# Projections that read their tokens alternately from two halves

## The chip, the cores and the metric

The kernel runs on one core of a Trainium2 chip. The metric is device time in microseconds (us). The engines are TensorE (PE, with its weight load PEld), VectorE (DVE), ScalarE (ACT), GpSimd (POOL) and SyncE (SP), which issues the DMAs. Matmuls read from SBUF and write to PSUM, which has eight banks; one bank holds 512 float32 columns on each of 128 partitions.

## The reference

Two layers of an encoder trunk on 256 tokens of width 2048, in float32. Layer 0 mixes tokens with RWKV-7 heads and an RG-LRU side by side; layer 1 uses sparse attention with low-rank queries and keys.

```python
for layer in range(DEPTH):
    if layer % 2 == 0:
        z = x @ ev_w_in[j]
        y_a = rwkv7_mix(z[..., :A_COLS], ...)
        y_b = rglru_mix(z[..., A_COLS:], ...)
        y = jnp.concatenate([y_a, y_b], axis=-1) @ ev_w_out[j]
    else:
        y = dsa_mix(x, od_w_in[j], ...) @ od_w_out[j]
    x = layer_norm(DN_ALPHA * x + y, ...)
    x = layer_norm(DN_ALPHA * x + conv_ffn(x, ...), ...)
    x = x + jax.nn.sigmoid(x @ ple_w_gate[layer]) * (p[layer] @ ple_w_proj[layer])
```

`rwkv7_mix` mixes each token with the one before it (`z + (token_shift(z) - z) * mu`), `rglru_mix` and `conv_ffn` run a causal convolution over four and three tokens. These are the places where the order of the tokens matters outside a matmul.

## The kernel before

Activations lie transposed: 128 features on the partitions, 256 tokens along the free axis (`S` = 256). A float32 value is split into a high part that fp32r holds and a residual, so an activation tile `hl` has 512 columns: high parts of tokens 0 to 255, then residuals of tokens 0 to 255 (`hl_split`, L135). Weights are split in the same way into `hi` and `lo` after each load (`wchunk`, L117): SP issues the load, ACT makes `hi`, DVE makes `lo`.

A product of one 128 x 128 weight block and one activation tile is made by `mm3` (L141) in one of two forms. The form with two matmuls (L149, L150) multiplies `hi` with all 512 columns and `lo` with the 256 high ones; the bank then holds two halves of 256 sums, which its reader adds. The form with three matmuls (`one=True`, L145 to L147) puts everything into one half. `gproj` (L171) runs over the blocks of one output block (16 for the width 2048, 44 for the feed-forward width), and `ordered` (L164) does the same in an order that `dodge` writes out for a few blocks (L169). All the large projections go through these: input and output projections of the mixers, the up and down projections of the feed-forward part (`ffn`, L376), the gate (`ple`, L464), the small projections of the attention layer (`small_proj`, L1345) and the projection of `p` (`ple_proj`, L427).

The banks are read by `evac` (L246: ACT copies one half to SBUF, DVE adds the other), `ln_set` and `ln_more` (L267, L276: DVE adds to the scaled residual stream), `ple_proj` (ACT scales), `ple` (a last tanh on ACT), `shifted` (L732: ACT scales by 1 - mu, DVE adds mu times the token before), `rglru` (L1023: ACT applies the last tap of the convolution and DVE the three others, all straight from the bank; later ACT applies Gelu to a second bank), `index_keys`, `low_rank` and `small_proj` in the attention layer (ACT copies).

In the even layer `stage1` and `stage2` of the RWKV heads are generators. A driver in `run` takes matmuls of other projections from `filler` whenever a stage yields, so that TensorE has work while short chains on DVE and ACT finish. Instructions run in the order of each engine's queue; semaphores that the tile framework places hold the dependencies. Attention's own products, the recurrent products of the RWKV heads and the block products of the RG-LRU are plain float32 matmuls that don't go through `mm3`.

Of the kernel before, what the change touches and what calls it, by code (L numbers as in the profile page):

```python
# [14 lines left out]
P = 128  # L15
D = 2048
S = 256
# [39 lines left out]
class Core:  # L57
# [77 lines left out]
    def hl_split(self, dst, src):  # L135
# [3 lines left out]
        nc.vector.tensor_tensor(dst[:, S:2 * S], src, dst[:, 0:S].bitcast(F32), op=ALU.subtract)  # L139

    def mm3(self, ps, hi, lo, hl, first, last, one=False):  # L141

        nc = self.nc
        if one:
            nc.tensor.matmul(ps[:, 0:S], hi, hl[:, 0:S], start=first, stop=False)  # L145
# [3 lines left out]
        nc.tensor.matmul(ps[:, 0:2 * S], hi, hl, start=first, stop=False)  # L149
        nc.tensor.matmul(ps[:, 0:S], lo, hl[:, 0:S], start=False, stop=last)  # L150

# [12 lines left out]
    def ordered(self, ps, hi, lo, hls, k0, order):  # L164

        for what, k in order[2 * k0:2 * k0 + 16]:
            c = slice((k - k0) * P, (k - k0 + 1) * P)
            out, w, x = (ps[:, 0:2 * S], hi, hls[k]) if what == "H" else (ps[:, 0:S], lo, hls[k][:, 0:S])
            self.nc.tensor.matmul(out, w[:, c], x, start=(what, k) == order[0], stop=(what, k) == order[-1], skip_group_check=True)  # L169
# [76 lines left out]
    def evac(self, ps, out):  # L246

        nc = self.nc
        t = self.t("ev")
        nc.scalar.copy(t, ps[:, S:2 * S])  # L250
        nc.vector.tensor_tensor(out, ps[:, 0:S], t, op=ALU.add)  # L251

# [14 lines left out]
    def ln_set(self, m, ps, hl):  # L267

        nc = self.nc
        s = self.sm[m] = self.ln_new(m)  # L270
        t = self.t("lnt")
        nc.vector.scalar_tensor_tensor(s, hl[:, 0:S].bitcast(F32), ALPHA, ps[:, 0:S], op0=ALU.mult, op1=ALU.add)
        nc.vector.scalar_tensor_tensor(t, hl[:, S:2 * S].bitcast(F32), ALPHA, ps[:, S:2 * S], op0=ALU.mult, op1=ALU.add)
        nc.vector.tensor_tensor(s, s, t, op=ALU.add)

    def ln_more(self, m, ps):  # L276

        s = self.sm[m]
        self.nc.vector.tensor_tensor(s, s, ps[:, 0:S], op=ALU.add)

# [146 lines left out]
    def ple_proj(self, l, wps, phl, half, pool=None):  # L427

        pps, pss = [], [None] * 2
        for m in range(8 * half, 8 * half + 8):  # L430
            wp = wps[m % 8 // 4]
            if pool is None:

                if m % 4 < 2:
                    pss[m % 2] = self.ps()
                ps, n = pss[m % 2], m % 4 // 2
            else:
                if m % 2 == 0:
                    ps = self.ps()
                n = m % 2  # L440
            pv = ps[:, n * S:(n + 1) * S]
            for k in range(2):
                o = ((m % 4) * 2 + k) * P
                self.mm3(pv, wp[0][:, o:o + P], wp[1][:, o:o + P], phl[k], k == 0, k == 1, True)
            if pool is None:
                t = self.t("sp")
                self.nc.scalar.mul(t, pv, 0.5)
                self.nc.sync.dma_start(self.spill[l][:, (m % 8) * S:(m % 8 + 1) * S], t)
            elif m % 2:
                pp = pool.tile([P, 2 * S], F32, tag="pp", name=self.nm("pp"), bufs=KD // 2)  # L450
                self.nc.scalar.mul(pp, ps, 0.5)
                pps += [pp[:, 0:S], pp[:, S:]]
        return pps
# [10 lines left out]
    def ple(self, l, pool, new, raws, emit):  # L464
# [7 lines left out]
        def finish(m, ps):  # L472
# [6 lines left out]
            if m == KD - 1:  # L479
                nc.scalar.activation(g, ps[:, 0:S], AF.Tanh, scale=0.5)  # L480
            else:
# [197 lines left out]
class Even:  # L679
# [343 lines left out]
    def rglru(self, j, yout):  # L1023
# [3 lines left out]
        xc = self.r1("xc")  # L1027
        A.activation(xc, ps[:, 0:S], AF.Identity, bias=k.v("bconv_b", j), scale=k.v("bconv3", j))
# [33 lines left out]
        g = self.r1("g")  # L1062
        A.activation(g, ps[:, 0:S], AF.Gelu_apprx_tanh)
        V.tensor_tensor(h, h, g, op=ALU.mult)
# [173 lines left out]
class Odd:  # L1238
# [31 lines left out]
    def index_keys(self):  # L1270
# [5 lines left out]
        z = k.t("kz")  # L1276
        A.copy(z, ps[:, 0:S])
        yield
# [28 lines left out]
    def low_rank(self, m0, n, gain, name, back=False):  # L1307
# [7 lines left out]
        for i in range(n):  # L1315
# [5 lines left out]
            z = zs[i]  # L1321
            A.copy(z, ps[:, 0:S])
            if i == 0:
# [21 lines left out]
    def small_proj(self, w, o, hls, out, scale=1.0):  # L1345
# [4 lines left out]
        for i in range(n):  # L1350
            k.mm3(ps, w[0][:, o + i * P:o + (i + 1) * P], w[1][:, o + i * P:o + (i + 1) * P], hls[i], i == 0, i == n - 1, True)
        nc.scalar.mul(out, ps[:, 0:S], scale)

# [263 lines left out]
```

## Time and profile before

| what | us |
|---|---|
| median of 3 runs | 2404.59 |
| lowest and highest | 2403.81 and 2405.13 |
| span of the profiled execution | 2404.5 |
| TensorE busy in it | 2382.8 |
| VectorE busy in it | 1773.9 |
| ScalarE busy in it | 1377.4 |

The even layer's mixer fills about the first 450 us, then come its output, the feed-forward part and the gate up to about 1340 us, the attention layer's mixer, and the second feed-forward part and gate up to the end. A line of the profile's list of groups gives the line of the kernel, the engine, the operation, the tile written and those read, the shape and the count; then the busy time in us, the mean duration of one in ns, and the engine's idle time just before them with what ended it. Durations of matmuls overlap, since matmuls are pipelined: how long one holds TensorE is read from the start of the next. L53 is the line of a helper through which many operations on DVE and ACT are issued, so these go by their tiles.

### The profile page before, as it was taken

Reading aid. Unit: us, or ns where it says so; the run is one execution under the profiler, and the core shown is the slowest. Engines: PE = TensorE matmul, PEld = TensorE weight load, DVE = VectorE, ACT = ScalarE, POOL = GpSimd, SP = SyncE. Lnnn points to the kernel's source line nnn. Section 1 sums busy time; section 2 is a strip of 40 time slices with the busy share of each in tenths; the row PEclk is TensorE's granted clock in tenths of the full one; section 3 lists DMA queues with packets and bytes.
Section 4 is the critical chain, followed back from the end, with each engine's and each line's share of the span. In section 5 each row is a group of like instructions: output and inputs, shape, how many; then the busy total and the mean of one; then the engine's idle time right before and its main releaser. Section 6 shows DMA issues by size and latency. Waiting matters only on the chain.

```text
span 2404.5 us, 40333 instructions
## 1 busy us (share of the span) xinstructions
PE 2382.8 (99%) x15064; PEld 2139.0 (89%) x15064; DVE 1773.9 (74%) x3598; ACT 1377.4 (57%) x2610; POOL 77.0 (3%) x73
## 2 busy tenths in 40 slices
PE   9999999999999999999999999999999999999999
PEld 8999999888888888888888998888888888888898
DVE  7788888887777777655579598887777777655587
ACT  6777776466555555443356567565555555444354
POOL 0011110000000000000000030000000000000000
PEclk9999999999999999999999999999999999999999
DMA  7444444556665666666666654646666666666665
GB/s 240 145 153 142 139 121 153 174 177 203 191 188 191 191 189 190 185 189 188 189 187 199 188 164 143 214 150 189 191 189 189 192 191 189 183 189 189 192 193 158
DMA packets 137588, 433.77 MB, mean 180 GB/s; under 512 B 16544, under 2 KB 29232, under 8 KB 137392
## 3 DMA queue, kind: packets, MB, share of 16 engines
q1 hardware_dynamic: 137392, 431.19, 57.8%
q8 instruction: 118, 1.93, 0.4%
q14 instruction: 78, 0.64, 0.1%
HBM read 426.65 MB, written 4.48 MB: 179 GB/s over the span
## 4 chain that ended last, share of the span: by engine, by line
PE 88%; DVE 4%; ACT 3%; DMA 3%; issue 1%; POOL 0%; SPq 0%; POOLq 0%; DVEq 0%; ACTq 0%
PE a L149 26%; PE pp L149 18%; PE a L150 13%; PE pp L150 9%; PE pp L145 4%; PE pp L146 4%; PE pp L147 3%; PE a L169 3%; PE a L875 2%; PE pp L169 1%; DMA raw<-evin 1%; ACT hi L53 1%; DVE lo L53 1%; DMA wr<-pg 1%; PE a L145 1%
## 5 line engine op out<-in xcount | busy, mean ns | idle before, releaser
L53 DVE TENSOR_TENSOR lo<-raw,hi 128x1024 fp32r<-128x1024 f32 (+3 forms) x1153 | 976.9, 862 | 464.6 <-ACT hi L53 462.5
L53 ACT CAST hi<-raw 128x1024 fp32r<-128x1024 f32 (+3 forms) x1153 | 840.3, 755 | 697.8 <-PE a L149 305.3
L149 PE MATMUL a<-x,hi 128*128 128x512 f32 x1768 | 619.1, 394 | 2.2 <-DVE x L333 2.2
L150 PE MATMUL a<-x,lo 128*128 128x256 f32 x1768 | 489.6, 277 | 0.0
L149 PEld LDWEIGHTS a<-x,hi 128*128 128x128 f32 x1768 | 331.3, 188 | 79.5 <-DVE x L333 2.9
L149 PE MATMUL pp<-x,hi 128*128 128x512 f32 x1112 | 391.6, 394 | 0.0
L150 PEld LDWEIGHTS a<-x,lo 128*128 128x128 f32 x1768 | 332.0, 188 | 0.3
L150 PE MATMUL pp<-x,lo 128*128 128x256 f32 x1112 | 308.0, 277 | 0.0
L149 PE MATMUL a<-g,hi 128*128 128x512 f32 x836 | 290.4, 394 | 0.0
L149 PEld LDWEIGHTS pp<-x,hi 128*128 128x128 f32 x1112 | 208.5, 188 | 48.5 <-ACT hi L53 0.2
L145 PE MATMUL pp<-x,hi 128*128 128x256 f32 x800 | 239.2, 300 | 1.5 <-ACT x L138 1.2
L150 PE MATMUL a<-g,lo 128*128 128x256 f32 x836 | 231.6, 277 | 0.0
L146 PE MATMUL pp<-x,hi 128*128 128x256 f32 x800 | 226.1, 283 | 0.9 <-DVE x L139 0.9
L147 PE MATMUL pp<-x,lo 128*128 128x256 f32 x800 | 225.9, 283 | 0.0
L392 DVE SCALAR_TENSOR_TENSOR cv<-u,vec_sb,cv 128x255 f32<-128x255 f32 x352 | 169.5, 482 | 64.1 <-ACT cv L389 58.2
L150 PEld LDWEIGHTS pp<-x,lo 128*128 128x128 f32 x1112 | 208.8, 188 | 0.2 <-DVE lo L53 0.2
L149 PEld LDWEIGHTS a<-g,hi 128*128 128x128 f32 x836 | 156.8, 188 | 36.5
L149 PE MATMUL pp<-g,hi 128*128 128x512 f32 x484 | 168.3, 394 | 0.0
L389 ACT ACTIVATE cv<-u,vec_sb 128x256 f32<-128x256 f32 x176 | 105.7, 601 | 93.0 <-DVE u L251 93.0
L150 PEld LDWEIGHTS a<-g,lo 128*128 128x128 f32 x836 | 156.8, 188 | 0.0
L145 PEld LDWEIGHTS pp<-x,hi 128*128 128x128 f32 x800 | 152.8, 191 | 2.9 <-ACT x L138 1.6
L146 PEld LDWEIGHTS pp<-x,hi 128*128 128x128 f32 x800 | 153.0, 191 | 2.1 <-DVE x L139 1.6
(439 smaller groups left out, 3734.9 us busy)
## 6 DMA issues: line engine op xcount, KB each, us to landing
raw<-up SPq DMA_DIRECT2D x347, 512.0 KB, 4.4
raw<-dn SPq DMA_DIRECT2D x160, 512.0 KB, 4.2
raw<-evin SPq DMA_DIRECT2D x85, 512.0 KB, 4.2
raw<-pg SPq DMA_DIRECT2D x54, 512.0 KB, 4.7
raw<-odout SPq DMA_DIRECT2D x32, 512.0 KB, 4.5
raw<-evout SPq DMA_DIRECT2D x16, 512.0 KB, 4.0
raw<-dn SPq DMA_DIRECT2D x32, 256.0 KB, 2.9
raw<-evout SPq DMA_DIRECT2D x16, 448.0 KB, 4.0
```

What stands on the lines that cost most here:

```text
L53: return getattr(self.eng, name)(*args, **kw)
L145: nc.tensor.matmul(ps[:, 0:S], hi, hl[:, 0:S], start=first, stop=False)
L146: nc.tensor.matmul(ps[:, 0:S], hi, hl[:, S:2 * S], start=False, stop=False)
L147: nc.tensor.matmul(ps[:, 0:S], lo, hl[:, 0:S], start=False, stop=last)
L149: nc.tensor.matmul(ps[:, 0:2 * S], hi, hl, start=first, stop=False)
L150: nc.tensor.matmul(ps[:, 0:S], lo, hl[:, 0:S], start=False, stop=last)
L169: self.nc.tensor.matmul(out, w[:, c], x, start=(what, k) == order[0], stop=(what, k) == order[-1], skip_group_check=True)
L389: nc.scalar.activation(y, u, AF.Identity, bias=self.v(f"cb{l}", j), scale=self.v(f"cw2{l}", j))
L392: nc.vector.scalar_tensor_tensor(y[:, d:], u[:, 0:S - d], self.v(f"cw{n}{l}", j), y[:, d:], op0=ALU.mult, op1=ALU.add)
L875: self.nc.tensor.matmul(ps[:, c * P:(c + 1) * P], lhs[:, c * P:(c + 1) * P], rhs(c), start=True, stop=True)
```

## The change

Three helpers give access patterns. `zip` makes a matmul read the 256 tokens of a half as 0, 128, 1, 129, and so on: the inner step is 128 elements with a count of two, the outer step one element. The tiles in SBUF keep their order. The matmul still writes its columns one after the other, so column 2b of a bank holds token b and column 2b + 1 token 128 + b. `unzip` reads a bank back in token order, all the even columns and then all the odd ones, and `nat` gives an SBUF tile the same shape.

```diff
+    def zip(self, ap):
+        if ap.shape[1] == S:
+            return ap.rearrange("p (q b) -> p b q", q=2)
+        return ap.rearrange("p (h q b) -> p h b q", h=2, q=2)
+    def unzip(self, ap):
+        return ap.rearrange("p (b q) -> p q b", q=2)
+    def nat(self, ap):
+        return ap.rearrange("p (q b) -> p q b", q=2)
...
-            nc.tensor.matmul(ps[:, 0:S], hi, hl[:, 0:S], start=first, stop=False)
-            nc.tensor.matmul(ps[:, 0:S], hi, hl[:, S:2 * S], start=False, stop=False)
-            nc.tensor.matmul(ps[:, 0:S], lo, hl[:, 0:S], start=False, stop=last)
+            nc.tensor.matmul(ps[:, 0:S], hi, z(hl[:, 0:S]), start=first, stop=False)
+            nc.tensor.matmul(ps[:, 0:S], hi, z(hl[:, S:2 * S]), start=False, stop=False)
+            nc.tensor.matmul(ps[:, 0:S], lo, z(hl[:, 0:S]), start=False, stop=last)
...
-        nc.tensor.matmul(ps[:, 0:2 * S], hi, hl, start=first, stop=False)
-        nc.tensor.matmul(ps[:, 0:S], lo, hl[:, 0:S], start=False, stop=last)
+        nc.tensor.matmul(ps[:, 0:2 * S], hi, z(hl), start=first, stop=False)
+        nc.tensor.matmul(ps[:, 0:S], lo, z(hl[:, 0:S]), start=False, stop=last)
...
-        nc.scalar.copy(t, ps[:, S:2 * S])
-        nc.vector.tensor_tensor(out, ps[:, 0:S], t, op=ALU.add)
+        nc.scalar.copy(self.nat(t), self.unzip(ps[:, S:2 * S]))
+        nc.vector.tensor_tensor(self.nat(out), self.unzip(ps[:, 0:S]), self.nat(t), op=ALU.add)
...
-        nc.vector.scalar_tensor_tensor(s, hl[:, 0:S].bitcast(F32), ALPHA, ps[:, 0:S], op0=ALU.mult, op1=ALU.add)
-        nc.vector.scalar_tensor_tensor(t, hl[:, S:2 * S].bitcast(F32), ALPHA, ps[:, S:2 * S], op0=ALU.mult, op1=ALU.add)
+        for o, c in ((s, slice(0, S)), (t, slice(S, 2 * S))):
+            nc.vector.scalar_tensor_tensor(self.nat(o), self.nat(hl[:, c].bitcast(F32)), ALPHA, self.unzip(ps[:, c]), op0=ALU.mult, op1=ALU.add)
...
-        nc.scalar.mul(out, ps[:, 0:S], self.omu[:, j:j + 1])
-        nc.vector.scalar_tensor_tensor(out[:, 1:], ps[:, 0:S - 1], k.v("mu", j), out[:, 1:], op0=ALU.mult, op1=ALU.add)
+        o, p, mu, h = k.nat(out), k.unzip(ps[:, 0:S]), k.v("mu", j), out[:, P:P + 1]
+        nc.scalar.mul(o, p, self.omu[:, j:j + 1])
+        nc.scalar.activation(h, ps[:, S - 2:S - 1], AF.Identity, scale=mu, bias=h)
+        nc.vector.scalar_tensor_tensor(o[:, :, 1:], p[:, :, 0:P - 1], mu, o[:, :, 1:], op0=ALU.mult, op1=ALU.add)
...
-        A.activation(xc, ps[:, 0:S], AF.Identity, bias=k.v("bconv_b", j), scale=k.v("bconv3", j))
+        u = k.t("u")
+        A.copy(k.nat(u), k.unzip(ps[:, 0:S]))
+        A.activation(xc, u, AF.Identity, bias=k.v("bconv_b", j), scale=k.v("bconv3", j))
         for n in range(3):
             d = 3 - n
-            V.scalar_tensor_tensor(xc[:, d:], ps[:, 0:S - d], k.v(f"bconv{n}", j), xc[:, d:], op0=ALU.mult, op1=ALU.add)
+            V.scalar_tensor_tensor(xc[:, d:], u[:, 0:S - d], k.v(f"bconv{n}", j), xc[:, d:], op0=ALU.mult, op1=ALU.add)
```

`ordered` takes `zip` in the same way, and the remaining readers (`ln_more`, `ple_proj`, the last tanh of `ple`, the Gelu of `rglru`, `index_keys`, `low_rank`, `small_proj`) take `nat` and `unzip` with nothing else changed. In `shifted` the token before token 128 is token 127, which lies in column 254 of the bank; the added one-column instruction on ACT handles it. In `rglru` an added ACT copy brings the bank into SBUF in token order, since the taps shift by one to three tokens.

More of the change, by code (lines that the diff above doesn't have):

```diff
@@ L139, in hl_split @@
         nc.vector.tensor_tensor(dst[:, S:2 * S], src, dst[:, 0:S].bitcast(F32), op=ALU.subtract)
+    def zip(self, ap):
[6 more added lines that the diff above has]
+        return ap.rearrange("p (q b) -> p q b", q=2)
     def mm3(self, ps, hi, lo, hl, first, last, one=False):
[L143 removed]
+        nc, z = self.nc, self.zip
         if one:
[L145 to L147 removed]
+            nc.tensor.matmul(ps[:, 0:S], hi, z(hl[:, 0:S]), start=first, stop=False)
+            nc.tensor.matmul(ps[:, 0:S], hi, z(hl[:, S:2 * S]), start=False, stop=False)
+            nc.tensor.matmul(ps[:, 0:S], lo, z(hl[:, 0:S]), start=False, stop=last)
             return
[L149 to L150 removed]
+        nc.tensor.matmul(ps[:, 0:2 * S], hi, z(hl), start=first, stop=False)
+        nc.tensor.matmul(ps[:, 0:S], lo, z(hl[:, 0:S]), start=False, stop=last)
     def dodge(self, j):
@@ L167, in ordered @@
             c = slice((k - k0) * P, (k - k0 + 1) * P)
-            out, w, x = (ps[:, 0:2 * S], hi, hls[k]) if what == "H" else (ps[:, 0:S], lo, hls[k][:, 0:S])
+            out, w, x = (ps[:, 0:2 * S], hi, self.zip(hls[k])) if what == "H" else (ps[:, 0:S], lo, self.zip(hls[k][:, 0:S]))
             self.nc.tensor.matmul(out, w[:, c], x, start=(what, k) == order[0], stop=(what, k) == order[-1], skip_group_check=True)
@@ L271, in ln_set @@
         t = self.t("lnt")
-        nc.vector.scalar_tensor_tensor(s, hl[:, 0:S].bitcast(F32), ALPHA, ps[:, 0:S], op0=ALU.mult, op1=ALU.add)
-        nc.vector.scalar_tensor_tensor(t, hl[:, S:2 * S].bitcast(F32), ALPHA, ps[:, S:2 * S], op0=ALU.mult, op1=ALU.add)
+        for o, c in ((s, slice(0, S)), (t, slice(S, 2 * S))):
+            nc.vector.scalar_tensor_tensor(self.nat(o), self.nat(hl[:, c].bitcast(F32)), ALPHA, self.unzip(ps[:, c]), op0=ALU.mult, op1=ALU.add)
         nc.vector.tensor_tensor(s, s, t, op=ALU.add)
     def ln_more(self, m, ps):
-        s = self.sm[m]
-        self.nc.vector.tensor_tensor(s, s, ps[:, 0:S], op=ALU.add)
+        s = self.nat(self.sm[m])
+        self.nc.vector.tensor_tensor(s, s, self.unzip(ps[:, 0:S]), op=ALU.add)
     def ln_stat(self, m):
@@ L446, in ple_proj @@
                 t = self.t("sp")
-                self.nc.scalar.mul(t, pv, 0.5)
+                self.nc.scalar.mul(self.nat(t), self.unzip(pv), 0.5)
                 self.nc.sync.dma_start(self.spill[l][:, (m % 8) * S:(m % 8 + 1) * S], t)
@@ L450, in ple_proj @@
                 pp = pool.tile([P, 2 * S], F32, tag="pp", name=self.nm("pp"), bufs=KD // 2)
-                self.nc.scalar.mul(pp, ps, 0.5)
+                self.nc.scalar.mul(pp.rearrange("p (n q b) -> p n q b", n=2, q=2), ps.rearrange("p (n b q) -> p n q b", n=2, q=2), 0.5)
                 pps += [pp[:, 0:S], pp[:, S:]]
@@ L479, in finish @@
             if m == KD - 1:
-                nc.scalar.activation(g, ps[:, 0:S], AF.Tanh, scale=0.5)
+                nc.scalar.activation(self.nat(g), self.unzip(ps[:, 0:S]), AF.Tanh, scale=0.5)
             else:
@@ L1062, in rglru @@
         g = self.r1("g")
-        A.activation(g, ps[:, 0:S], AF.Gelu_apprx_tanh)
+        A.activation(k.nat(g), k.unzip(ps[:, 0:S]), AF.Gelu_apprx_tanh)
         V.tensor_tensor(h, h, g, op=ALU.mult)
@@ L1276, in index_keys @@
         z = k.t("kz")
-        A.copy(z, ps[:, 0:S])
+        A.copy(k.nat(z), k.unzip(ps[:, 0:S]))
         yield
@@ L1321, in low_rank @@
             z = zs[i]
-            A.copy(z, ps[:, 0:S])
+            A.copy(k.nat(z), k.unzip(ps[:, 0:S]))
             if i == 0:
@@ L1351, in small_proj @@
             k.mm3(ps, w[0][:, o + i * P:o + (i + 1) * P], w[1][:, o + i * P:o + (i + 1) * P], hls[i], i == 0, i == n - 1, True)
-        nc.scalar.mul(out, ps[:, 0:S], scale)
+        nc.scalar.mul(k.nat(out), k.unzip(ps[:, 0:S]), scale)
     def scores(self):
```

## The prediction

> **What bounds the kernel now.** I read the head of the page first, then its chain of work that ended last.
>
> ```profile
> span 2404.5 us, 40333 instructions
> PE 2382.8 (99%) x15064; PEld 2139.0 (89%) x15064; DVE 1773.9 (74%) x3598; ACT 1377.4 (57%) x2610; POOL 77.0 (3%) x73
> ...
> PE 88%; DVE 4%; ACT 3%; DMA 3%; issue 1%; POOL 0%; SPq 0%; POOLq 0%; DVEq 0%; ACTq 0%
> ```
>
> TensorE is busy for 99% of the span and makes up 88% of the chain. A busy PE row need not be PE at its peak, so the next view is the stretches of time, with the busy time of PE, PEld, DVE, ACT and POOL, their instruction counts and the granted clock.
>
> ```profile
> 0.00:450.00 450.00, 437.73 (x3419) 422.07 (x3420) 371.14 (x1198) 317.82 (x855) 48.99 (x48) 1.00 0.50 158
> 450.00:1340.00 890.00, 886.33 (x5237) 779.48 (x5237) 639.51 (x1057) 479.61 (x770) 2.39 (x4) 1.00 0.61 189
> ...
> 700.00:800.00 100.00, 100.00 (x579) 87.43 (x578) 72.18 (x109) 57.19 (x90) 0.00 (x0) 1.00 0.60 190
> ```
>
> The clock is 1.00 throughout, and in a steady stretch of the feed-forward part 579 matmuls fill 100 us with no idle time: 172.7 ns for one, 345.4 ns for a pair (one of 512 columns, one of 256). So the time is the sum of the spacings of matmuls, and whatever changes that spacing goes to the end one for one. Even in the first 450 us, where DVE is 82% busy (371.14 of 450), PE is idle for only 12.3 us. The timeline (start, duration, engine, line) shows the spacing itself.
>
> ```profile
> 800.33 0.40 PE L149 MATMUL pp<-x,hi 128*128 128x512 f32 x1
> 800.34 0.19 PEld L150 LDWEIGHTS pp<-x,lo 128*128 128x128 f32 x1
> ...
> 800.57 0.28 PE L150 MATMUL pp<-x,lo 128*128 128x256 f32 x1
> 800.57 0.19 PEld L149 LDWEIGHTS pp<-x,hi 128*128 128x128 f32 x1
> 800.68 0.39 PE L149 MATMUL pp<-x,hi 128*128 128x512 f32 x1
> ...
> 2395.95 0.28 PE L145 MATMUL a<-x,hi 128*128 128x256 f32 x1
> ...
> 2396.31 0.28 PE L145 MATMUL a<-x,hi 128*128 128x256 f32 x1
> ```
>
> A 512-column matmul holds PE for about 0.23 us (800.33 to 800.57), a 256-column one for 0.11 us. In the form with three 256-column matmuls, one round takes 0.36 us, 120 ns each. The weights of the next matmul start loading as a matmul starts, so two streams leave SBUF together.
>
> **Is there an excess in that spacing?** The list of groups, different shapes apart, has fp32r matmuls (L149, L150) beside plain float32 ones (L875, L1426), which take two passes of slower columns; the timeline has the spacing of L875.
>
> ```profile
> L149 PE MATMUL a<-x,hi 128*128 128x512 f32 x1768 | 619.1, 394 | 2.2 <-DVE x L333 2.2
> L150 PE MATMUL a<-x,lo 128*128 128x256 f32 x1768 | 489.6, 277 | 0.0
> ...
> L875 PE MATMUL a<-Y,HT 128*128 128x128 f32 x192 | 25.5, 275 | 1.7 <-ACT Y L53 1.7
> L1426 PE MATMUL a<-kh,qh 128*128 128x256 f32 x32 | 9.6, 380 | 0.0
> ...
> 217.38 1.05 PE L875 MATMUL a<-Dd,ET 128*128 128x128 f32 x8
> 218.26 1.06 PE L875 MATMUL a<-R,Dd 128*128 128x128 f32 x8
> ```
>
> Plain float32: 380 - 275 = 105 ns for 128 more columns, 0.82 ns a column. Eight L875 records take 0.88 us, 110 ns each, of which 105 are columns, so a matmul costs 5 ns beside its columns. fp32r: 394 - 277 = 117 ns for 256 more columns, 0.457 ns a column. Half of 0.82 is 0.41, and I take that (my choice: one step where float32 takes two) as the rate without hindrance. Then a pair would need 768 x 0.41 + 2 x 5 = 325 ns, against 346: an excess of 21 ns. A single 256-column matmul would need 110 ns, against 120: an excess of 10 ns. The Trainium skill, page "TensorE: Matmul & The Clock Gate", section "Back-to-back issue gap", gives N/2.4 + 2.5 ns, 216 ns at 512 columns; the trace has about 230 for fp32r here, so that formula alone does not describe these matmuls.
>
> **The change, part by part.** First, every projection matmul reads its moving columns with steps of 512 bytes. These are the instructions of L149, then L169, then L145 (L146 and L147 have as many), over the whole span:
>
> ```profile
> 0.00:2404.50 2404.50, 1670.70 (x4800) 1.00 0.58 180
> ...
> 0.00:2404.50 2404.50, 104.83 (x576) 1.00 0.58 180
> ...
> 0.00:2404.50 2404.50, 341.68 (x1152) 1.00 0.58 180
> ```
>
> That is 4800 + 288 = 5088 pairs and 3 x 1152 = 3456 singles, or 5088 x 768 + 3456 x 256 = 4.79 million columns. No instruction is added to PE. Nothing in this trace reads a moving operand with such a step, so this cost is bounded. From below: the whole excess goes, 5088 x 21 + 3456 x 10 = 107 + 35 = 142 us gained. From above, the only read with a long inner step is DVE's reduction over steps of 64 bytes, against a plain one of the same 256 elements:
>
> ```profile
> L53 DVE TENSOR_REDUCE y<-dblk 128x64 f32<-128x256 f32 x8 | 4.7, 589 | 0.0
> ...
> L1463 DVE TENSOR_REDUCE sm<-L 128x1 f32<-128x256 f32 x16 | 6.5, 408 | 0.0
> ```
>
> That is 181 ns more, 0.71 ns an element (part of it may be the 64 results instead of one). At 0.71 ns on 4.79 million columns the loss is 3400 us. Between ends so far apart I go to the nearest rows, PE's own. The excess appears where two streams, moving columns and weights, are each read straight through at full rate, and is almost absent in L875, where the columns come at half the rate beside equal weight loads. It looks like the two streams getting in each other's way, and an alternating order is one way to part them. I take 115 of the 142 us: 0.41 is rounded (0.005 ns on 4.79 million columns is 24 us).
>
> Second, whoever reads a bank takes every second column. Rows touched most:
>
> ```profile
> L250 ACT COPY ev<-a 128x256 f32<-128x256 f32 x129 | 47.1, 365 | 6.4 <-PE a L150 6.4
> ...
> L251 DVE TENSOR_TENSOR u<-a,ev 128x256 f32<-128x256 f32 x110 | 46.0, 418 | 1.2 <-ACT ev L250 1.2
> ...
> L272 DVE SCALAR_TENSOR_TENSOR s<-x,pp 128x256 f32<-128x256 f32 x37 | 15.4, 417 | 7.7 <-PE pp L150 7.5
> ```
>
> The bounds are nothing and again 0.71 ns an element, 182 ns on each; I take nothing, the nearest being a step of 8 bytes, far from 64. Even the upper bound adds one ACT and one DVE piece of 0.18 us to each output block of 16 pairs, 5.5 us, where DVE is 72% and ACT 57% busy: PE's own work hides it, and without that cover it would cost 0.18 us for each of some 200 blocks, 36 us. At four layer-norm boundaries and at the last activation nothing covers it: 5 x 2 x 0.18, under 2 us.
>
> Third, instructions added in the even layer: one ACT instruction on one column for each of 27 shifted blocks (8 x 3 + 3), and one ACT copy of a bank for each of 8 convolutions, whose four later readers then read SBUF.
>
> ```profile
> L1464 ACT ACTIVATION_READ_ACCUMULATOR pr<-L,sm 128x1 f32 x32 | 6.7, 210 | 0.0
> ...
> L1028 ACT ACTIVATE xc<-pp,vec_sb 128x256 f32<-128x256 f32 x8 | 4.5, 561 | 0.0
> ...
> L53 ACT ACTIVATE kf<-ta,half 128x256 f32<-128x256 f32 x8 | 4.8, 600 | 0.1
> ```
>
> 27 x 0.21 + 8 x 0.365 + 8 x (0.600 - 0.561) = 5.7 + 2.9 + 0.3 = 8.9 us of ACT, in 450 us where it works 318. The one-column instruction also stands between the scaling on ACT and the shifted add on DVE, so the add waits 0.21 us more; behind it on DVE stand the weight residuals that feed PE. The filler projections cover this, as they do the present chain; uncovered it is 27 x 0.21 = 5.7 us. I take 2 us for it and 2 for the uncovered ends. No DMA is added or moved, and no queue is passed.
>
> Sum: 2404.5 - 115 + 4 = 2293.5; rounded to **2293 us**. The span and the median of the runs (2404.59) differ by 0.1 us, so no further correction is made.
>
> **The rivals.** *The step costs PE a fetch for each column* (the other side). Four neighbouring columns share 16 bytes; in the new order no two successive columns lie near each other, so if the stream lives on fetching several at once it falls to the rate of the slower columns, 0.82 ns. A pair then takes 768 x 0.82 + 10 = 640 ns, 294 more; a single 215 ns, 95 more: 5088 x 0.294 + 3456 x 0.095 = 1496 + 328 = 1824 us, and the time is about 4230 us. The place is every projection. It decides as soon as a column costs 0.03 ns (142 us over 4.79 million) more than that excess gives back. For it speaks the reduction at 589 ns; against it, that DVE's reduction is another port with more results. The Trainium skill, page "SBUF — State Buffer", section "Specifications (TRN2)", has this as a rule: 16-byte lines, full bandwidth only with two or more hits in a line, a penalty for each crossing; no run here shows it for PE.
>
> *The stream takes columns one by one anyway.* Then the order is indifferent, the excess belongs to the change of weights, and only the readers' 0 to 8 us remain: 2404 to 2412, about 2407. For it speaks that the excess is 10 ns on each matmul, whether 256 or 512 columns long (21 a pair). The Trainium skill, "TensorE: Matmul & The Clock Gate", section "Step-by-step: what each phase is for", says that the weights come through a read port of their own and take nothing from the moving stream. By that there is no conflict to part; the trace doesn't decide it, since L875 differs in rate too.
>
> *Half of the excess goes:* 2404.5 - 71 + 4, about 2338; it belongs to the first case.
>
> **How the numbers follow.** Forecast (all or part of the excess goes): 0.52, with a range of its own from 2265 to 2355. Indifferent: 0.20, of which 0.14 within 0.2% (4.8 us, about what a measurement of this kernel can tell from no change) and 0.06 beyond it. A fetch for each column: 0.28. So faster 0.52, same 0.14, slower 0.34. Forecast and indifference hold 0.72 together, not enough, so the range has to reach the third case: 2265 to 4250. It leaves out what would lie nearer to the 0.71 ns bound.
>
> **What would show it.** Right: the 512-column matmul starts the next within 0.22 us instead of 0.23, a round of three in 0.33 instead of 0.36, 100 us hold some 610 matmuls instead of 579. Rival one: both spacings near double, and DVE's and ACT's shares of the span fall by half. Rival two: the spacing stays at 346 ns a pair. Readers: L250's 365 and L251's 418 ns stay, or grow toward 547 and 600. The prediction is wrong if PE's spacing grows at all, or if PE begins to wait in the first 450 us for the banks' readers.

## The result, and the profile after

The changed kernel takes 2308.17 us (median of 4 runs, 2306.36 to 2310.11), against 2404.86 us for the kernel before in the same series: a ratio of 0.9598 with a 95% interval from 0.9584 to 0.9611, 96.7 us less. The forecast was 2293 us: the side and most of the size are right, 15 us are missing.

The head of the page of the kernel after, and the engines' shares in its chain of work that ended last:

```profile
span 2304.6 us, 40382 instructions
...
PE 2269.6 (98%) x15064; PEld 2106.0 (91%) x15064; DVE 1771.7 (77%) x3598; ACT 1385.3 (60%) x2646; POOL 81.2 (4%) x73
...
PE 80%; DVE 9%; ACT 5%; DMA 4%; issue 1%; POOL 1%; SPq 0%; POOLq 0%; DVEq 0%; ACTq 0%
```

As many matmuls keep TensorE busy for 113 us less. The busy time of DVE and ACT hardly moved (1773.9 to 1771.7, 1377.4 to 1385.3), but DVE's part in the chain rose from 4% to 9%: somewhere the chain now runs through it instead of TensorE. Where, the stretches suggest (columns as before: window, PE, PEld, DVE, ACT, POOL, granted clock, DMA share, GB/s):

```profile
0.00:450.00 450.00, 430.83 (x3449) 413.17 (x3450) 376.81 (x1211) 330.22 (x898) 53.25 (x48) 1.00 0.50 159
700.00:800.00 100.00, 100.00 (x613) 91.97 (x612) 76.46 (x115) 60.64 (x96) 0.00 (x0) 1.00 0.65 202
```

In the feed-forward part 613 matmuls fill 100 us where 579 did: 2 x 100 / 613 = 326.3 ns a pair, 19.1 less than the 345.4 of before, with no idle time. In the even layer's mixer only 30 matmuls more (3449 for 3419) fit into 450 us, and TensorE is now idle for 19.2 us instead of 12.3. The timeline shows both forms of projection, pairs (L163, L164) and rounds of three (L159 to L161):

```profile
800.31 0.38 PE L163 MATMUL a<-x,hi 128*128 128x512 f32 x1
...
800.53 0.27 PE L164 MATMUL a<-x,lo 128*128 128x256 f32 x1
...
800.64 0.38 PE L163 MATMUL a<-x,hi 128*128 128x512 f32 x1
...
2294.99 0.28 PE L159 MATMUL a<-x,hi 128*128 128x256 f32 x1
2295.10 0.28 PE L160 MATMUL a<-x,hi 128*128 128x256 f32 x1
2295.21 0.28 PE L161 MATMUL a<-x,lo 128*128 128x256 f32 x1
2295.32 0.28 PE L159 MATMUL a<-x,hi 128*128 128x256 f32 x1
```

From start to start: 0.22 us for 512 columns, 0.11 for 256, and 0.33 for a round of three, which took 0.36. So both forms run faster where the stream is unbroken. What came of it at the end is seen by comparing the start of the n-th matmul in the two traces (both have 15064, in nearly the same order):

| matmul | start before, us | sooner by, us |
|---|---|---|
| 3300, end of the even mixer | 429 | 4.0 |
| 4000 | 548 | 7.6 |
| 8000, late in the first layer | 1233 | 45.8 |
| 9500, end of the attention mixer | 1453 | 50.9 |
| 14000 | 2228 | 92.5 |
| end of span | 2404.5 | 99.9 |

From 4000 to 8000 the gain is 38.2 us, for some 1920 pairs and 140 single matmuls: about 19 ns a pair, as in the window. In the even mixer, with some 2000 matmuls of the form of three in it, 8 ns each would be 16 us; 4 came.

The readers of the banks and the added instructions, from the list of groups of the kernel after, and from the view of the line of the added one-column instruction (minimum, median, maximum in ns):

```profile
L264 ACT COPY ev<-a 128x256 f32<-128x256 f32 x129 | 47.2, 366 | 3.7 <-PE a L164 3.7
L265 DVE TENSOR_TENSOR u<-a,ev 128x256 f32<-128x256 f32 x110 | 46.1, 419 | 0.0
L287 DVE SCALAR_TENSOR_TENSOR s<-x,pp 128x256 f32<-128x256 f32 x37 | 15.4, 417 | 3.7 <-PE pp L164 3.7
...
L753 ACT ACTIVATE r<-pp,r,vec_sb x8: 343/356/357, 40.5 to 351.1; 128x1 f32<-128x1 f32 x8
```

366, 419 and 417 ns against 365, 418 and 417: taking every second column of a bank costs these readers nothing.

### The profile page after: what moved, and what is told of

It is laid out like the page before. It is cut to its first block, busy times and chain, and to the rows that moved or that the text cites. A ratio compares the mean times of both kernels' runs of the same rounds, so it can differ in the third digit from the quotient of the medians.

```text
span 2304.6 us, 40382 instructions
## 1 busy us (share of the span) xinstructions
PE 2269.6 (98%) x15064; PEld 2106.0 (91%) x15064; DVE 1771.7 (77%) x3598; ACT 1385.3 (60%) x2646; POOL 81.2 (4%) x73
## 4 chain that ended last, share of the span: by engine, by line
PE 80%; DVE 9%; ACT 5%; DMA 4%; issue 1%; POOL 1%; SPq 0%; POOLq 0%; DVEq 0%; ACTq 0%
PE a L163 25%; PE pp L163 18%; PE a L164 12%; PE pp L164 9%; PE a L183 3%; DVE lo L53 2%; PE pp L159 2%; PE pp L160 2%; PE pp L161 2%; ACT hi L53 2%; DMA raw<-evin 2%; PE pp L183 1%; PE a L891 1%; DMA raw<-up 1%; DMA raw<-evout 1%
## 5 line engine op out<-in xcount | busy, mean ns | idle before, releaser
L163 PE MATMUL a<-x,hi 128*128 128x512 f32 x1768 | 585.7, 382 | 2.0 <-DVE x L347 2.0
L164 PE MATMUL a<-x,lo 128*128 128x256 f32 x1768 | 481.4, 273 | 0.0
L163 PEld LDWEIGHTS a<-x,hi 128*128 128x128 f32 x1768 | 334.0, 189 | 49.2 <-DVE x L347 2.4
L163 PE MATMUL pp<-x,hi 128*128 128x512 f32 x1112 | 371.2, 382 | 0.3 <-DVE x L347 0.2
L164 PEld LDWEIGHTS a<-x,lo 128*128 128x128 f32 x1768 | 339.4, 192 | 0.1
L164 PE MATMUL pp<-x,lo 128*128 128x256 f32 x1112 | 302.9, 273 | 0.0
L163 PE MATMUL a<-g,hi 128*128 128x512 f32 x836 | 274.4, 382 | 0.0
L163 PEld LDWEIGHTS pp<-x,hi 128*128 128x128 f32 x1112 | 210.2, 189 | 30.5 <-ACT pp L465 0.6
L159 PE MATMUL pp<-x,hi 128*128 128x256 f32 x800 | 233.8, 293 | 2.5 <-DVE la L754 1.9
L164 PE MATMUL a<-g,lo 128*128 128x256 f32 x836 | 227.9, 273 | 0.0
L160 PE MATMUL pp<-x,hi 128*128 128x256 f32 x800 | 221.5, 277 | 2.0 <-DVE x L139 2.0
L161 PE MATMUL pp<-x,lo 128*128 128x256 f32 x800 | 220.8, 276 | 1.6 <-DVE lo L53 1.6
L164 PEld LDWEIGHTS pp<-x,lo 128*128 128x128 f32 x1112 | 213.4, 192 | 0.2 <-DVE lo L53 0.2
L163 PEld LDWEIGHTS a<-g,hi 128*128 128x128 f32 x836 | 158.0, 189 | 22.0
L164 PEld LDWEIGHTS a<-g,lo 128*128 128x128 f32 x836 | 160.5, 192 | 0.0
L163 PE MATMUL pp<-g,hi 128*128 128x512 f32 x484 | 159.1, 382 | 0.0
L159 PEld LDWEIGHTS pp<-x,hi 128*128 128x128 f32 x800 | 154.3, 193 | 3.8 <-DVE la L754 2.1
```

The costliest lines, as they stand in the source:

```text
L159: nc.tensor.matmul(ps[:, 0:S], hi, z(hl[:, 0:S]), start=first, stop=False)
L160: nc.tensor.matmul(ps[:, 0:S], hi, z(hl[:, S:2 * S]), start=False, stop=False)
L161: nc.tensor.matmul(ps[:, 0:S], lo, z(hl[:, 0:S]), start=False, stop=last)
L163: nc.tensor.matmul(ps[:, 0:2 * S], hi, z(hl), start=first, stop=False)
L164: nc.tensor.matmul(ps[:, 0:S], lo, z(hl[:, 0:S]), start=False, stop=last)
```

## The experiments

Two questions are open: why the alternating order is faster, and where the 15 us stayed. For the first I ran streams of matmuls by themselves, for the second parts of the change.

**The order of the columns.** Groups of 64 fp32r matmuls with eight weight blocks in turn; the moving operand is one tile of 512 columns read in another order in each group.

```diff
+two = x.rearrange("p (h q b) -> p h b q", h=2, q=2)     # also q=4, 32, 64, 128
+big = x.rearrange("p (q b) -> p b q", q=2)
+pair = x.rearrange("p (q b t) -> p b q t", q=2, t=2)    # also t=4, 8
+for i in range(64):
+    mm(ps, W(i), two, start=True, stop=True)
```

> Leaves out the whole computation: one fp32r activation tile (128x512) and eight weight blocks are loaded, and TensorE runs groups of 64 matmuls of 512 columns, each group on a line of its own, each matmul with the next of eight 128-column weight blocks, straight from one another. Only the order in which the 512 moving columns are read differs: straight; two halves of 256 in turn (step 512 bytes, as in the change); four quarters (256 bytes); steps of 32, 16 and 8 bytes; two halves of 512 in turn (1 KB); pairs, quads and eights of neighbours taken in turn from two halves of 512; backwards; straight again. Theory A (the moving stream and the weight load run into each other when the columns are read straight, and any order that leaves the 16 bytes of the last column at each step avoids it): straight about 231 ns between starts, every step of 16 bytes or more about 217, step 8 bytes in between, pairs and quads between, backwards like straight. Theory B (it is the distance of 512 bytes, two places of SBUF that can be read in turn): only the 512-byte and 1 KB orders, and perhaps pairs to eights, come to 217; the steps of 256 bytes and less stay at 231 or become slower. Rival C (each column from another 16 bytes costs a fetch, and the change gains for another reason): the long steps are slower here than straight.

From its list of groups: straight (L45), the order of the changed kernel (L47), four places (L49), 128 places 8 bytes apart (L55), two places 1 KB apart (L57), pairs of neighbours from two places in turn (L59); 32 and 64 places, groups of four and of eight, and backwards took 431, 460, 250, 243 and 233 ns. The spacing of the starts is (busy time - mean) / 63, to about 1 ns.

```profile
L45 PE MATMUL bank<-x,w 128*128 128x512 f32 x64 | 14.7, 389 | 0.0
L47 PE MATMUL bank<-x,w 128*128 128x512 f32 x64 | 14.0, 379 | 0.0
L49 PE MATMUL bank<-x,w 128*128 128x512 f32 x64 | 18.3, 451 | 0.0
L55 PE MATMUL bank<-x,w 128*128 128x512 f32 x64 | 29.2, 632 | 0.0
L57 PE MATMUL bank<-x,w 128*128 128x512 f32 x64 | 14.0, 379 | 0.0
L59 PE MATMUL bank<-x,w 128*128 128x512 f32 x64 | 21.9, 513 | 0.0
```

Straight 227 ns, two places 216 at either distance; four places 283, steps of 8 bytes 453, pairs 340. Two places are the exception, not the start of a trend: theory A, which had every step of 16 bytes or more near 217, fails, and rival C is right for the other long steps but not for the two places.

**Narrower weights, fewer columns, plain float32.** The same streams with 64 and 32 columns of weights, so that the weight stream has less to move, and with 256 and 128 moving columns.

```diff
+mm(ps[0:64], W(i)[:, 0:64], x, start=True, stop=True)     # straight, then two; also 32
+mm(ps[:, 0:256], W(i), x[:, 0:256], start=True, stop=True)
+mm(ps[:, 0:256], wraw(i), xraw[:, 0:256], start=True, stop=True)   # float32
```

> Leaves out the whole computation: groups of 64 matmuls as in the run on orders, now with other weight loads. Straight columns with 128, 64 and 32 weight columns; alternating columns with 64 and 32; straight and alternating columns with weights read at a step of 32 bytes; straight columns with weights at a step of 8 bytes; 256 columns and 128 columns, straight and alternating; the same weight block each time; plain float32 with 256 columns, straight and alternating. Theory A (straight columns run into the weight load): the excess of about 15 ns over 216 falls with the weight columns, to about 8 at 64 and 4 at 32, changes when the weights are read at another step, and alternating columns show none of it at any width; plain float32 shows no difference between the orders. Theory D (a fixed cost at each change of weights): the excess stays about 15 ns with 64 and 32 weight columns. Theory E (a cost of reading neighbours, per column): 512 straight columns have twice the excess of 256, whatever the weights.

Straight with 64 (L49) and 32 weight columns (L51), alternating with 32 (L55), 256 moving columns straight and alternating (L63, L65), 128 straight (L67), 512 straight with the same block each time (L71), float32 straight and alternating (L73, L75, two records for each matmul):

```profile
L49 PE MATMUL bank<-x,w 128*64 128x512 f32 x64 | 14.9, 392 | 0.0
L51 PE MATMUL bank<-x,w 128*32 128x512 f32 x64 | 15.0, 394 | 0.0
L55 PE MATMUL bank<-x,w 128*32 128x512 f32 x64 | 14.0, 379 | 0.0
...
L63 PE MATMUL bank<-x,w 128*128 128x256 f32 x64 | 7.8, 283 | 0.0
L65 PE MATMUL bank<-x,w 128*128 128x256 f32 x64 | 7.3, 275 | 0.0
L67 PE MATMUL bank<-x,w 128*128 128x128 f32 x64 | 7.3, 274 | 0.0
L71 PE MATMUL bank<-x,w 128*128 128x512 f32 x64 | 14.8, 390 | 0.0
...
L73 PE MATMUL bank<-raw 128*128 128x256 f32 x128 | 27.8, 379 | 0.0
L75 PE MATMUL bank<-raw 128*128 128x256 f32 x128 | 35.1, 437 | 0.0
```

With a quarter of the weight columns the straight stream is no faster (232 ns, not 227), and the alternating one stays at 216. With the same block loaded each time the straight one takes 228, and the alternating order, with as many changes of weights, has no excess; so a cost at each change (theory D) is out as well. For 512 columns, then, the excess does not come from the weight load: the prediction's guess falls. 256 columns go from 120 to 112 ns, and 128 columns take 111, so that below 256 the columns no longer set the spacing. For 256 columns the guess is not excluded: there the weight load sat idle for 0.1 us of its whole group, and narrower weights were run with 512 columns alone. The excess is not simply one per column either (theory E), 11 ns at 512 columns and 8 at 256. Weights read with a step of 32 bytes slow both orders (246 and 242 ns), so the weight load is not without effect; but it is not what the alternating order relieves. Plain float32 loses by the same order: 216 ns a record become 273.

**The distance of the two places.** Was it that the two places lie in different parts of SBUF?

```diff
+apart = x[:, 0:2 * d].rearrange("p (q b) -> p b q", q=2)[:, 0:128]   # d = 128 to 384 columns
+inner = x.rearrange("p (h q b) -> p h b q", h=h, q=2)                # 512 down to 32 bytes
```

> Leaves out the whole computation: as the run on orders, 64 matmuls a group, weights of 128 columns read straight. Two columns in turn with 512 columns in all, from blocks whose halves lie 512, 256, 128, 64 and 32 bytes apart; two columns in turn with 256 columns in all, 512, 528, 576, 640, 768, 1024 and 1536 bytes apart; four places in turn and eight places in turn, each 512 bytes from the next; straight columns that start at byte 0, 256 and 16 of the tile. The runs before gave 216 ns for two places 512 bytes or 1 KB apart, 283 for four places 256 bytes apart. Theory F (SBUF answers faster when successive reads go to two different stretches of 512 bytes; the distance decides): two places give 216 at 512 bytes, clearly more than 227 at 256 and below; at 256 columns 112 for 512, 1024 and 1536 bytes, more than 112 for some of the distances between; four and eight places at 512 bytes give 216 too. Theory G (the number of places decides: two in turn is the good case): two places give 216 at every distance, four places at 512 bytes about 283, eight worse. Start of the straight columns: 227 in both theories, unless the start alone shifts it.

Two places 32 bytes apart (L52), two places 1536 bytes apart with 256 columns (L66), four places 512 bytes apart (L68), eight places (L70):

```profile
L52 PE MATMUL bank<-x,w 128*128 128x512 f32 x64 | 14.0, 379 | 0.0
...
L66 PE MATMUL bank<-x,w 128*128 128x256 f32 x64 | 7.3, 275 | 0.0
L68 PE MATMUL bank<-x,w 128*128 128x512 f32 x64 | 18.3, 448 | 0.0
L70 PE MATMUL bank<-x,w 128*128 128x512 f32 x64 | 31.4, 668 | 0.0
```

Every distance tried, from 32 to 512 bytes with 512 columns and from 512 to 1536 bytes with 256, gives the same spacing, 216 and 112 ns; four places give 283, eight 487. The distance made no difference (theory G); what else is it about two? Straight columns that start 16 bytes into the tile took 232 ns instead of 227, and 227 when they start 256 bytes in; that the start alone shifts them is not explained.

**What the two places have that others lack.** One theory left: a fetch takes a piece of 16 bytes (four columns), and the first, third, fifth ... column of the stream goes through one lane, the second, fourth ... through another; a lane is at full speed when its columns follow one another within a piece. Its rival: any two places are fast, because the fetches of one hide behind the other.

```diff
+inner(64)   # 0,4,1,5,2,6,3,7, 8,12,...
+inner(128)  # 0,2,1,3, 4,6,5,7, ...
+swapped     # 1,0,3,2, ...
+hop = x.rearrange("p (q b s) -> p b q s", q=2, s=s)[:, :, :, 0]   # two places, every s-th column
+one2 = x[:, 0:512:2]
```

> Leaves out the whole computation: 64 matmuls a group as in the runs on orders. Now: halves of blocks of 8 columns in turn (16 bytes apart: 0, 4, 1, 5, ...); of blocks of 4 (0, 2, 1, 3, all in the same 16 bytes); neighbours exchanged (1, 0, 3, 2); two places 516 and 520 bytes apart (their 16-byte pieces change at different columns); two far places that each go on by 2, 3 and 4 columns (8, 12, 16 bytes); one place that goes on by 2; 256 straight columns; last the kernel's own round of 512 and 256 columns, straight and alternating. The runs before: two places in turn 216 at any distance from 32 bytes up, pairs of neighbours in turn 340, quads 250, four places 283, straight 227. Theory L (columns are fetched in two lanes, one for the even and one for the odd ones; a lane is fast as long as it takes one neighbour after the other, and straight order makes each lane skip one): blocks of 8: 216; blocks of 4 and exchanged neighbours: 227 or more; 516 and 520 bytes: 112 as at 512; two places by 2: between 216 and 227 or as straight; two places by 3 and 4 (256 columns): near 200, as the lanes leave their 16 bytes at each step; one place by 2 (256 columns): near 200. Theory N (it is enough that two successive columns lie in different 16-byte pieces): two places by 2, 3 and 4 stay at 216 and 112, one place by 2 near 120. The round: about 346 straight, 327 alternating; if the straight one is shorter here, the rest of the kernel takes a part in the 346.

Blocks of eight (L47) and of four columns (L49), 512 columns each; then 256 columns: two places by steps of three (L59) and four (L61) columns, one place by two (L63):

```profile
L47 PE MATMUL bank<-x,w 128*128 128x512 f32 x64 | 14.0, 379 | 0.0
L49 PE MATMUL bank<-x,w 128*128 128x512 f32 x64 | 14.7, 390 | 0.0
...
L59 PE MATMUL bank<-x,w 128*128 128x256 f32 x64 | 11.2, 342 | 0.0
L61 PE MATMUL bank<-x,w 128*128 128x256 f32 x64 | 14.7, 405 | 0.0
L63 PE MATMUL bank<-x,w 128*128 128x256 f32 x64 | 14.7, 405 | 0.0
```

Counted by how many columns a lane takes from a piece before it goes to the next, and put for 512 columns:

| order | columns a piece in a lane | ns |
|---|---|---|
| two places; blocks of 8 | 4 | 216 |
| straight; neighbours exchanged; blocks of 4; two places by 2 | 2 | 227 |
| two places by 3 (173 x 2) | 4/3 | 346 |
| two places by 4; one place by 2 (226.6 x 2) | 1 | 453 |

The last three rows are close to 453 divided by the count (227, 340, 453), the first is limited at 216 by something else. This division was found in the results: theory L as recorded had about 200 for the last two rows' streams of 256 columns, which took 173 and 227. The rival would have kept 112 ns for 256 columns at steps of three and four. So what helps is that each of the two interleaved streams goes on by one column. That there are two lanes is inferred from spacings alone, and some orders don't fit by size: by this count pairs would take 453 (340 measured), four places 453 (283), 32 places 453 (431), eight places 453 (487), groups of four neighbours 227 (250). Nor do 256 straight columns: half of 227 is 113, and they took 120. So of the 8 ns that the order takes off a 256-column matmul the count accounts for about 2; the rest, 6 of the 19 ns of a pair, has no explanation here.

The kernel's own round of 512 and 256 columns took 353 ns straight and 327 alternating. The second is the kernel's 326; the first is more than the kernel's 345 and than 227 + 120, which is not explained.

**The matmuls' half of the change, and the readers' half.** The first has the matmuls alternate and leaves all readers of before, the second the reverse.

```diff
-        nc.tensor.matmul(ps[:, 0:2 * S], hi, hl, start=first, stop=False)
+        nc.tensor.matmul(ps[:, 0:2 * S], hi, z(hl), start=first, stop=False)
```

> The matmuls read alternately as in the changed kernel, but the readers of the banks are those of before (straight, no added ACT instructions); tokens come out in the wrong order, so the output is not the reference's. Theory A with a loss in the even layer through the added ACT work and the longer chain: about 2297 us, 11 us better than the changed kernel, with the gain in the first 450 us near 15 us instead of 4. Rival (the even layer is held by the chains on DVE and ACT that were there already): about 2306 us, the gain in the first 450 us stays near 4 us.

> The matmuls read straight as before, but the readers and the added ACT instructions are those of the changed kernel; tokens come out in the wrong order, so the output is not the reference's. If the readers' steps and the added instructions are hidden, 2404 to 2408 us (the prediction has 4 us for them); if they cost what the gain lacks, 2412 to 2418 us, with the loss in the first 450 us.

The matmuls alone: 2304.06 us against 2405.15, ratio 0.9579 (0.9563 to 0.9595), 101.1 us less. The readers alone: 2409.03, ratio 1.0015 (1.0005 to 1.0024), 3.9 us more. Their sum, 97.2 us less, is the change's own 96.7: the halves add up. The first 450 us of the matmuls alone:

```profile
0.00:450.00 450.00, 430.32 (x3454) 414.29 (x3455) 376.27 (x1213) 320.54 (x863) 48.95 (x48) 1.00 0.50 159
```

With the readers of before, TensorE is as idle (19.7 us) as with the new ones. So the readers' new work is not what it waits for. The recorded rival (2306 us, about 4 us gained in the first 450) came out, not the 2297 of theory A; for the readers, 2409 lies between the two recorded ranges, next to the one in which their work is hidden.

**Pairs alone, rounds of three alone.** Each puts the other form back as it was before; the edit against the changed kernel of the first begins so:

```diff
-            nc.tensor.matmul(ps[:, 0:S], hi, z(hl[:, 0:S]), start=first, stop=False)
+            nc.tensor.matmul(ps[:, 0:S], hi, hl[:, 0:S], start=first, stop=False)
```

> Only the pairs of matmuls (512 and 256 columns) read alternately, with unzip in the two readers of such banks; the form with three matmuls of 256 columns and its readers stay as before, and so no instruction is added. The reference's output. If the gains add up stage by stage (19.6 ns on each of 5088 pairs, all of it on PE's path): about 100 us less, 2305 us, and the three-matmul form then brings next to nothing in the changed kernel. If the three-matmul form has a part in the gain of 97 us: 2312 to 2325 us.

> Only the form with three matmuls reads alternately, with its readers and the added ACT instructions; the pairs and their readers stay as before. The reference's output. By spacing alone 8 ns on each of 3456 matmuls would give 28 us, 2377 us. If chains on DVE and ACT hold the even layer and the attention mixer, only the matmuls outside them count: 2396 to 2403 us.

Pairs alone: 2314.16 us, ratio 0.9619 (0.9603 to 0.9635), 91.0 us less. Rounds of three alone: 2399.38, ratio 0.9979 (0.9969 to 0.9989), 5.8 us less. Together 96.8. The first 450 us with the rounds alone:

```profile
0.00:450.00 450.00, 431.61 (x3441) 412.09 (x3442) 375.60 (x1210) 328.93 (x895) 53.27 (x48) 1.00 0.50 159
```

22 matmuls more than before, and 6.1 us less busy: most of what TensorE saves, it then waits. At matmul 3300, the rounds alone are 2.6 us ahead of before. The pairs alone are 2.6 us behind there, where hardly any of them has run: in that trace the granted clock was 0.5 in two stretches of 3.41 us (from 12.8 and 91.3 us), by an estimate up to 3.4 us lost.

**Who sets the pace in the even layer?** If it is DVE, taking work from DVE there must let the gain through. This kernel is the changed one without the residuals of the weights in the even layer.

```diff
-            lo = self.wpool.tile([P, n], F32R, tag="lo", name=self.nm("lo"), bufs=6)
+            lo = hi if self.skip else self.wpool.tile([P, n], F32R, tag="lo", name=self.nm("lo"), bufs=6)
...
-            V.tensor_tensor(lo[:, i:i + w], raw[:, i:i + w], hi[:, i:i + w].bitcast(F32), op=ALU.subtract)
+            if not self.skip:
+                V.tensor_tensor(lo[:, i:i + w], raw[:, i:i + w], hi[:, i:i + w].bitcast(F32), op=ALU.subtract)
```

> The changed kernel, but from the first RWKV stage to the end of the even layer's loop the residuals of the weights aren't made: the matmuls that read them read the high parts instead, and DVE loses some 370 subtractions of 0.42 us (150 us of 360). The output is not the reference's. TensorE's instructions, their number and their order stay. Theory H (in the even layer the gain is kept down by DVE: PE waits for chains that queue behind the weight residuals there): PE's idle time in the first 450 us falls from 19 us to 8 or less, and the time to 2290 to 2297 us. Rival (the chains themselves, their hops between ACT, DVE, PE and POOL, or the loads, are too long for the shorter filler): 2303 to 2309 us as the changed kernel.

The other one keeps all work and cuts each weight load of the even layer into two pieces instead of four, so that DVE and ACT make fewer and longer ones.

```diff
-CUT = 4
+CUT = 2
```

> The changed kernel with the weight tiles of the even layer split in two pieces instead of four: the same DVE and ACT work in fewer, longer instructions. The reference's output. If the 2 to 3 us between the two runs with permuting writers come from this: 2304 to 2306 us, the fastest version with the reference's output. Otherwise 2308 us as the changed kernel.

The first 450 us without the residuals, then with two pieces:

```profile
0.00:450.00 450.00, 437.51 (x3529) 424.89 (x3530) 272.49 (x849) 332.52 (x907) 32.71 (x48) 0.99 0.52 162
```

```profile
0.00:450.00 450.00, 431.51 (x3475) 415.88 (x3476) 371.03 (x1026) 314.82 (x704) 50.76 (x48) 1.00 0.51 160
```

Without the residuals: 2294.77 us, ratio 0.9537 (0.9521 to 0.9553). DVE falls from 377 to 272 us, TensorE's idle time from 19.2 back to 12.5, and matmul 3300 starts 15.4 us sooner than before instead of 4.0, close to the 16 that the faster rounds could give. The time is within what theory H had recorded, the idle time is not (8 us or less). That speaks for DVE as what holds back the rest, and does not prove it: what the kernel before would gain by the same removal was not run, so 15.4 is no exact share. With two pieces: 2303.6 us, ratio 0.9578 (0.9563 to 0.9592), matmul 3300 sooner by 7.2. That is the fastest kernel here that computes everything; the changed one stood at 0.9598 (0.9584 to 0.9611), so the intervals overlap and the order of the two is not certain.

**Permuting at the writers instead.** The activations are written to SBUF in the order that brings the sums out in token order, so that no bank's reader changes.

```diff
+    def put(self, ap):
+        return ap.rearrange("p (q b) -> p b q", q=2)
...
-        nc.scalar.copy(dst[:, 0:S], src)
-        nc.vector.tensor_tensor(dst[:, S:2 * S], src, dst[:, 0:S].bitcast(F32), op=ALU.subtract)
+        h, l, src = self.put(dst[:, 0:S]), self.put(dst[:, S:2 * S]), self.tok(src)
+        nc.scalar.copy(h, src)
+        nc.vector.tensor_tensor(l, src, h.bitcast(F32), op=ALU.subtract)
```

> All projection matmuls read alternately, but whoever writes an activation tile puts token 2b at place b and token 2b + 1 at place 128 + b, so that a bank holds the tokens in their order and its readers stay as before; no ACT instruction is added (only the one tile that is also a stationary operand keeps its order, and its one reader undoes it). The reference's output. If writes and reads at these steps cost what straight ones cost, as the run with the matmuls alone: 2301 to 2306 us, some 4 us less than the changed kernel. Rival: ACT and DVE write more slowly at these steps (hl_split and ln_apply 0.1 us longer or more), 2310 us or more.

> As the run with permuting writers, and the weight tiles of the even layer are split in two pieces of 512 columns instead of four of 256, which takes 0.3 us of DVE's time (4 x 421 to 2 x 684 ns) from each of some 50 tiles there, 16 us of 370. The reference's output. Theory H (in the even layer DVE's throughput keeps the gain down): 4 to 10 us less than the run with permuting writers. Rival (it is the length of single chains, and longer pieces stand in their way): the same or slower.

The writers: 2319.26 us, ratio 0.9641 (0.9628 to 0.9654). With two pieces as above: 2316.66, 0.9633 (0.962 to 0.9646), 2.6 us less where theory H had 4 to 10, and no clear difference. The groups of the kernel with the writers:

```profile
L149 ACT CAST g<-cv 128x256 fp32r<-128x256 f32 x88 | 58.9, 669 | 6.8 <-DVE cv L422 6.6
L150 DVE TENSOR_TENSOR g<-cv,g 128x256 fp32r<-128x256 f32 x88 | 54.9, 623 | 0.0
...
L359 ACT ACTIVATE x<-s,vec_sb 128x256 fp32r<-128x256 f32 x64 | 46.9, 758 | 25.0 <-DVE s L356 18.1 <-DVE x L360 6.8
L360 DVE SCALAR_TENSOR_TENSOR x<-s,vec_sb,x 128x256 fp32r<-128x256 f32 x64 | 42.5, 684 | 6.7 <-ACT x L359 5.7
```

The same casts and subtractions of the changed kernel, which writes in a row:

```profile
L139 DVE TENSOR_TENSOR g<-cv,g 128x256 fp32r<-128x256 f32 x88 | 36.9, 420 | 0.0
L138 ACT CAST g<-cv 128x256 fp32r<-128x256 f32 x88 | 35.5, 404 | 7.1 <-DVE cv L409 6.9
```

The layer norm's writers (L359, L360) took 506 and 484 ns there. The order is free at the banks and dear at these writers: 265 ns more for 256 values on ACT, 203 on DVE. Reading a tile so ordered is not what costs: the step that only reads it into the layer norm (L299, `s<-x,pp`) takes 425 ns where it took 417. This kernel is 11 us behind the changed one. In the trace the loss comes not in the even mixer (matmul 3300 is sooner by 3.5 us against 4.0) but after it (matmul 9500 by 39.9 against 50.9); that all of it is the writes' was not tested by itself.

## Why the prediction was right or wrong

*The spacing is the time.* Right for the streaming parts: 19.1 ns on each of 5088 pairs is 97 us, and the pairs alone gave 91.0. Wrong for the first 450 us. There the prediction took TensorE's 12.3 us of idle time as a sign that it set the pace; but an engine with little idle time may have another close behind it, and DVE at 371 of 450 us, with short chains, was that as far as the kernel without residuals shows it. The idle time grew to 19.2.

*The size of the excess.* Right: 326.3 ns a pair measured where the line of the prediction gave 325, 112 ns a single where it gave 110, 613 matmuls in 100 us where it gave 610. The floor, half the float32 column rate, held: 256 float32 columns take 216 ns a record, and so do 512 alternating fp32r columns. The rate of 0.457 ns a column that it was set against did not hold: it came from the mean durations, while the spacing of straight fp32r streams grows by 107 ns from 256 to 512 columns, 0.418 a column. The Trainium skill, page "TensorE: Matmul & The Clock Gate", section "Back-to-back issue gap", gives N/2.4 + 2.5 ns for the gap of isolated matmuls, 215.8 ns at 512 columns and 109.2 at 256. Here the alternating stream meets it at 512 (216) and is above it at 256 (112), where the straight ones took 227 and 120.

*The step that failed* is the first term of the sum in its part for the singles. All 3456 were counted at 10 ns, 35 us, of which 115/142, 28 us, were to come out. The rounds of three alone gave 5.8 us. The pairs, 107 us by the bound and 87 by the same share, gave 91.0. So the gain missed by 15 us because about 22 us too much stood on the singles, made up by 4 on the pairs and by the 4 us for readers and added work, which are already in the 5.8. Of the 3456 singles 2075 stand in the even mixer: at 8 ns each that is 16.6 us, of which 2.6 came in the trace of the rounds alone. There the gain is lost behind DVE, as far as the kernel without residuals bears it out.

*The reason* was wrong for the 512-column matmuls. Moving columns and weights were said to get in each other's way; with a quarter of the weight columns the excess is no smaller. It goes with the order of the columns themselves. For 256 columns the reason was not tested. The same reason would have spoken for four places (283 ns) or eight (487), which are slower than straight, so it was partly luck that the side came out as forecast. The size followed from the floor and not from the reason.

*The readers at nothing:* right, 366 and 419 ns. *The added ACT work:* the one-column instruction takes 0.35 us, not 0.21, so 27 x 0.35 = 9.5 us instead of 5.7, mostly covered; the readers' half costs 3.9 us, 4 had been taken.

*The rivals.* "A fetch for each column" did not decide here, but its price is real: one place by steps of two columns takes 226.7 ns for 256 columns, 0.89 ns a column, where the rival had 0.82. The Trainium skill, page "SBUF — State Buffer", section "Specifications (TRN2)", asks for two or more hits in a 16-byte line; taken of successive columns it would forbid the changed order, in which no two successive columns share a line, and the trace disagrees with that reading. Counted in each of two interleaved streams it comes close in the orders of the table: one hit 453 ns, two 227, though four are faster still, 216. "The order is indifferent" fell with the first window, and "half of the excess" too: 19.1 of 21 ns went.

*TensorE waiting for the banks' readers,* named as a sign against the forecast, did not come: it waits more, but just as much with the readers of before.

## What to carry to other kernels

A stream of fp32r matmuls with 256 or 512 moving columns may be read from two places in turn, each going on by one column: 5 to 7% off the spacing of such matmuls here, at any distance tried (32 to 1536 bytes). Measure four places, pairs, other steps and other types before using them, since those tried took up to 115% longer than straight. Undo the order where the sums are read from PSUM, which was free, not where the activations are written; and count the gain only in stages where no other engine is close behind TensorE. (That it was DVE in the even mixer rests on one run.)

## What the hardware showed besides

Plain float32 matmuls lose by the order that helps fp32r (273 against 216 ns a record). A DVE or ACT instruction that writes fp32r values alternately to two places 512 bytes apart took about half as long again on DVE (420 to 623 ns) and two thirds longer on ACT (404 to 669). And after a stretch in which TensorE idles, its clock can dip. Two stretches of the changed kernel, in which the clock of before was 1.00:

```profile
25.00:35.00 10.00, 8.06 (x58) 7.71 (x57) 8.68 (x41) 7.07 (x24) 0.00 (x0) 0.88 0.84 296
470.00:500.00 30.00, 27.64 (x192) 25.83 (x192) 26.28 (x66) 19.11 (x51) 0.69 (x1) 0.94 0.58 182
```

In each the granted clock was 0.5 for 3.41 us (from 32.6 and from 483.2 us), by which TensorE, busy throughout, loses an estimated 1.7 us. In the 3.41 us just before, TensorE was busy for only 0.43 and 0.44 of the time; of all stretches of that length, laid end to end from there over 2 to 2299 us, these were the two least busy, and the next (0.60, from 384.2 us) brought no dip. The profiled span of before has no dip. That the idle time brings them was not tested by itself, and the total doesn't show them: two executions of the changed kernel with a mean clock of 1.000 took 2306.88 and 2310.11 us, the one with 0.998 took 2306.36.

Open remain the orders that the two lanes don't explain by size, the 256-column matmul's excess among them, and why the straight stream grows slightly slower with narrower weights. Writing the sums to the bank in another order was not tried.
